# Turning the modulation rows of a two-block transformer kernel to columns once per eight steps

## The chip, the cores and the metric

The kernel runs on one core of one Trainium2 chip. The metric is the device time of one execution in microseconds (us); three executions were timed. Five engines work side by side: TensorE (PE, with its weight loads shown apart as PEld), VectorE (DVE), ScalarE (ACT), GpSimd (POOL) and SyncE (SP), which issues all the DMAs that matter here.

## What is computed

Block 1 has two layers over two streams, x (256 tokens) and ctx (256 tokens), each token 1024 wide. Each layer first makes six vectors of 1024 numbers from a conditioning vector; they scale, shift and gate the layer's two halves. There is one such set for each stream:

```
mx = jnp.split((silu_c @ w_mod[l] + b_mod[l])[:, None, :], N_MOD, axis=-1)
mc = jnp.split(silu_cc @ w_mod[l] + b_mod[l], N_MOD, axis=-1)
zx = modulate(rms_norm(x, norm1_g[l]), mx[0], mx[1]) @ w_in[l]
zc = modulate(rms_norm(ctx, norm1_g[l]), mc[0], mc[1]) @ w_in[l]
...
x = x + mx[2] * mixer_rest(fx, gx, attn_x, l)
hx = modulate(rms_norm(x, norm2_g[l]), mx[3], mx[4])
x = x + mx[5] * channel_mlp(hx, l)
```

`w_mod[l]` is 1024 x 6144, so per layer this product reads 25 MB of weights for only two rows of results (c and c_ctx). Between these lines stand an attention over eight heads, a Fourier mix, a convolution and an MLP. Block 2 (three mixers, a cross attention and an FFN) follows; it has no modulation.

## The kernel before

**Activations** lie with features on the 128 partitions and tokens along the free dimension. A large product goes block by block: 128 output features by 512 tokens, over eight k-tiles of 128, each in three passes (`wh`, `wh`, `wl`), because the weights and the activations are split into two parts each. ACT makes the high part of a weight block (`wh<-raw`), DVE the low part (`wl<-raw,wh`). Weight chunks of 512 KB land in four slots named `raw`, which the modulation weights share.

**Modulation** (`modulation`) is a generator of 24 steps per layer. A step is 128 features of two of the six vectors (256 columns in all), and eight steps make a pair of vectors, numbered r = 0, 1, 2. Here the weights are the moving operand: for each k-tile, a stationary `cs[:, k, :]` of 32 columns (columns 0 and 1 hold silu(c) and silu(c_ctx), the rest are zero) multiplies 256 columns of `raw`. The k-tiles go to four column groups of the array, so the partial sums of c and c_ctx lie on rows 32g and 32g + 1 of the accumulator `md`, half of a PSUM bank; the two halves alternate from step to step. A step's work is 8 matmuls of the program (16 in the trace, since fp32 goes in two passes), named `md<-raw,cs`. Then comes its **end**: ACT copies the half to `mrow` (`mrow<-md`), PE multiplies `mrow` as the stationary operand by the selector `sel`, which sums the four partial sums and turns rows to columns (`md<-cst_a,mrow`, 2 matmuls of the program, 4 in the trace), and DVE adds the bias (`mod<-md,vec`). The end writes into the half of `md` that it came from, and the step after next reuses that half. An end is written out after the next step's products.

**Order.** Ten steps are placed by hand around layer 0's first norm. From then on `weave` picks, by a model of when each engine is free, the next piece of several generators: keys and values, queries, attention, Fourier, convolution, input projection and, last, the filler, which is the modulation (in layer 1 alternating with the memory's keys and values for block 2). The traced program then goes through a list scheduler, which moves instructions again. `need_mod` forces the steps that are left before a vector is used: `need_mod(l, 2)` ahead of the output projection, and `need_mod(1, 0)` ahead of the last quarter of layer 0's MLP.

All engine instructions are recorded by one helper, so the profile gives every one of them line L238, and groups are told apart by tile names.

Of the kernel before, what the change touches and what calls it, by code (L numbers as in the profile page):

```python
# [11 lines left out]
F32 = mybir.dt.float32  # L12
# [15 lines left out]
# ------------------------------------------------------------------ layouts  # L28


def pack_w(w, kt, mc):
    """[kt*128, M] -> [M/mc, 128, mc/128 * kt * 128]: chunks that load contiguously, output block by block."""
    m = w.shape[1]
    return np.ascontiguousarray(
        w.reshape(kt, P, m // mc, mc // P, P).transpose(2, 1, 3, 0, 4).reshape(m // mc, P, kt * mc)
    )


def cols(v):
    """A vector of n*128 -> [128, n]."""  # L40
    return v.reshape(-1, P).T


def feat(a):
    """[T, D] -> [128, D/128, T]."""
    return a.T.reshape(-1, P, a.shape[0]).transpose(1, 0, 2)


def constants():
# [3 lines left out]
    sel = np.zeros((P, 2))  # L53
    for i in range(2):
        sel[i::32, i] = 1.0
# [88 lines left out]
INS = "ckv kr g0 a0 cq0 cq1 g1 a1 zf0 zf1".split()  # order of the blocks of w_in  # L144


def layout(i):
    """All device arrays, laid out; and where each small vector lies."""
# [72 lines left out]
# ------------------------------------------------------------------ program  # L221


TICK = 10.24 / 3  # of the PE's activity monitor, in us


class Engine:
    """An engine whose instructions the model of the core notes as they are issued."""
# [13 lines left out]
class Pool:  # L242
    """A tile pool whose slots' reuse the model notes."""
# [19 lines left out]
class Core:  # L263
    """The core, with a model of when each engine gets to what has been issued, in us.

    It serves only to choose the order in which work that does not depend on each other is traced."""
# [3 lines left out]
    TAIL = {"pe": 0.19, "dve": 0.16, "act": 0.18, "pool": 0.2, "dma": 2.0}  # until others see an end  # L270

    def __init__(self, nc):
# [3 lines left out]
        self.columns = {}  # tick of the PE's activity monitor -> columns counted  # L276
        self.used = {}    # tile -> end of its last use
        self.seen = {}    # tile -> accesses: box, end, engine, whether written
        self.last = 0.0   # the latest end since it was set to 0
        self.gaps = {k: [] for k in self.clock}  # when an engine waits, which later work may use  # L280
# [5 lines left out]
    def box(ap):  # L286
        """The first and last partition and element that an access touches."""
# [4 lines left out]
    def product(self, start, name, n, rows, cols, f32):  # L292
        """How long a product takes: the PE runs at half its rate after a tick with too few columns."""
# [28 lines left out]
    def after(self, ap):  # L322
        """When what has been issued so far has written ap."""
# [7 lines left out]
    def cooling(self):  # L331
        """Whether the PE has too few columns in this tick so far to run at its full rate in the next."""
# [3 lines left out]
    def place(self, key, ready, held):  # L336
        """When an instruction starts that could at ready: in the first gap that holds it, or behind the last."""
# [47 lines left out]
class Chain:  # L385
    """Work that is traced in steps: a generator that stops before products that wait for other engines.

    It yields the tiles that the next product waits for, nothing if that is all of the step, or a chain that has to
    end first. A chain that is mostly the DVE's (dve) goes on when the DVE has nothing else."""
# [6 lines left out]
class Squares:  # L396
    """Sums of squares over the features of tiles that come one by one: all but the last are added up on the way."""
# [18 lines left out]
    def sums(self, ones="ones"):  # L416
        """-> PSUM, the sums on each partition."""
# [7 lines left out]
class Early:  # L425
    """A norm's input before the norm, x times the scale of its features: both parts, tile by tile.

    The first products of a norm's output go on these; their sums take the norm's factor of each token (r) at the
    end, and with it the product of the shift."""
# [16 lines left out]
    def width(self, n):  # L446
        """How many columns its products of n tokens have: one stream's take the shifts along."""
        return n if self.shift is None or self.n > T else n + 2

    def shifts(self, blocks, pss):  # L450
        """The products of the shift with blocks of weights."""
# [33 lines left out]
class Prog:  # L485
# [28 lines left out]
    def later(self, tile, after):  # L514
        """Have the load of a tile wait for after: what is needed first goes first."""
# [23 lines left out]
    def banks(self, name, **bufs):  # L539
        """PSUM's banks, by use."""  # L540
# [5 lines left out]
    def temps(self, name, nhl, ntmp, nt):  # L546
        """Slots for plain activations ([128, nt]) and for activations' parts."""
# [10 lines left out]
    # ---- weights: load, split into the part that one pass carries and the rest  # L558
    @contextmanager
    def weights(self, name, nraw, wraw, nw=3, side="left"):  # L560
        """Slots for weights as loaded and for their parts."""
# [4 lines left out]
    def norms(self, name, n, side="left"):  # L566
        """Slots for norms of n tokens."""
# [14 lines left out]
    def wsplit(self, src, kt, f, wide=P, own=None):  # L582
        """-> (k, j) -> the two parts of the 128 x wide block of k-tile k and output block j."""
# [31 lines left out]
    def mm3(self, out, lh, ll, rh, rl, start, stop, **kw):  # L615
        """One K-tile of an fp32 product: three passes over exact parts."""
# [5 lines left out]
    def jobs(self, w, kt, mc, rhs, n, evac, chunks=None, m0=0, lead=0, kg=1, own=None, early=None, more=0, lead2=0,  # L622
             tag="mm"):
        """out^T[m] = sum_k W[k, m]^T act^T[k]; rhs: k -> (hi, lo). The first chunks (lead) go through k together,
        those of an Early and more of them on its tiles, and then lead2 ones.
# [1753 lines left out]
```

## Time and profile before

| | us |
|---|---|
| median of three executions (1748.15 to 1751.82) | 1751.02 |
| span of the profiled execution, first to last instruction | 1750.8 |
| PE busy in that span | 1667.3 |
| DVE busy | 1158.8 |
| ACT busy | 853.1 |
| mean granted TensorE clock, share of full speed | 0.962 |

The profiled execution has its span alone; no separate time for it is on record, and its span lies within the three times. It divides into stages: the start with the first norm (0 to 78 us), layer 0's projection and attention (78 to 252), its output projection and MLP (252 to 654), layer 1's projection and attention (654 to 820), the memory, output projection and MLP of layer 1 (820 to 1070), the mixers of block 2 (1070 to 1400), and the rest. Stage borders are rounded.

### The profile page before, as it was taken

How to read it: one execution, taken by the hardware profiler on the slowest of the kernel's cores; microseconds unless marked ns; L12 is line 12 of the kernel's file. 1: busy time of each engine (PE TensorE's matmuls, PEld its weight loads, DVE VectorE, ACT ScalarE, POOL GpSimd, SP SyncE). 2: the span in 40 equal slices, each digit the busy share in tenths (PEclk: the TensorE clock that was granted, in tenths of full speed). 3: DMA queues.
4: the chain of work that ended last, by engine and by line, in shares of the span. 5: the costliest groups of instructions: out<-in, count | busy, mean ns of one | idle time of the engine just before them, and what ended most of it. 6: DMA issues, size and time to landing. Idle time of an engine off the chain costs nothing.

```text
span 1750.8 us, 29987 instructions
## 1 busy us (share of the span) xinstructions
PE 1667.3 (95%) x12072; PEld 1429.8 (82%) x12072; DVE 1158.8 (66%) x2155; ACT 853.1 (49%) x1485; POOL 81.1 (5%) x74
## 2 busy tenths in 40 slices
PE   5899999999999998999999998899999999999997
PEld 3666668788888886767999997797888899999997
DVE  4686547743444366884679667787853868788864
ACT  4426764441323245466564446542334746666643
POOL 0000001000000011000100001011000001010000
PEclk8989999999999998989999998999988999999999
DMA  8743562233333335752756564332211475345553
GB/s 276 236 150 126 180 205 85 85 97 96 96 97 96 115 98 168 238 168 70 223 150 185 184 187 149 106 105 66 67 61 49 137 250 192 112 154 192 167 164 105
DMA packets 69403, 248.94 MB, mean 142 GB/s; under 512 B 7696, under 2 KB 13072, under 8 KB 65424
## 3 DMA queue, kind: packets, MB, share of 16 engines
q1 hardware_dynamic: 69264, 247.03, 44.2%
q8 instruction: 95, 1.56, 0.4%
q14 instruction: 44, 0.36, 0.1%
HBM read 242.80 MB, written 4.19 MB: 141 GB/s over the span
## 4 chain that ended last, share of the span: by engine, by line
PE 83%; DVE 8%; DMA 4%; ACT 4%; issue 1%; POOL 0%; SPq 0%; DVEq 0%; ACTq 0%
PE mm L238 63%; PE ax L238 11%; PE md L238 3%; PE sc L238 3%; PE fx L238 3%; DVE wl L238 2%; DMA raw<-w_in 1%; ACT wh L238 1%; DMA raw<-w_mod 1%; DVE tmp L238 1%; DVE y L238 1%; ACT L238 1%; DVE hl L238 1%; DMA x<-xc 0%; DVE x L238 0%
## 5 line engine op out<-in xcount | busy, mean ns | idle before, releaser
L238 PE MATMUL mm<-hl,wh 128*128 128x256 f32 (+2 forms) x3856 | 867.5, 320 | 15.0 <-DVE rw_in L238 7.6
L238 PEld LDWEIGHTS mm<-hl,wh 128*128 128x128 f32 x3856 | 645.5, 194 | 76.1 <-issue 8.7
L238 ACT CAST wh<-raw 128x1024 fp32r<-128x1024 f32 (+1 forms) x353 | 360.8, 1024 | 558.1 <-PE mm L238 434.3
L238 PE MATMUL mm<-hl,wl 128*128 128x256 f32 (+1 forms) x1928 | 613.4, 319 | 3.9 <-DVE wl L238 3.8
L238 DVE TENSOR_TENSOR wl<-raw,wh 128x1024 fp32r<-128x1024 f32 (+1 forms) x353 | 422.3, 1198 | 223.9 <-ACT wh L238 221.8
L238 PEld LDWEIGHTS mm<-hl,wl 128*128 128x128 f32 x1928 | 372.8, 193 | 30.4 <-DVE wl L238 6.8
L238 PE MATMUL mm<-y,wh 128*128 128x256 f32 x928 | 176.5, 290 | 7.1 <-DVE early L238 2.6
L238 PEld LDWEIGHTS mm<-y,wh 128*128 128x128 f32 x928 | 147.7, 194 | 10.3 <-DVE early L238 3.0
L238 PE MATMUL mm<-y,wl 128*128 128x256 f32 x464 | 133.1, 287 | 0.0
L238 DVE SCALAR_TENSOR_TENSOR x<-mm,mod,x 128x256 f32<-128x256 f32 x120 | 54.3, 480 | 117.9 <-PE mm L238 117.8
L238 POOL TENSOR_TENSOR sq<-sq,sq 128x256 f32<-128x256 f32 (+1 forms) x48 | 59.9, 1249 | 899.7 <-ACT sq L238 899.4
L238 PEld LDWEIGHTS mm<-y,wl 128*128 128x128 f32 x464 | 89.7, 193 | 0.6 <-issue 0.5
L238 PE MATMUL md<-raw,cs 128*32 128x256 f32 x768 | 62.6, 424 | 20.0 <-DMA raw<-w_mod 11.4
L238 PE MATMUL mm<-hid,wh 128*128 128x512 f32 x256 | 80.7, 397 | 0.0
L238 DVE SCALAR_TENSOR_TENSOR acc<-u,vec,acc 128x512 f32<-128x512 f32 (+1 forms) x120 | 73.2, 614 | 2.2
L238 ACT ACT_TABLE_LOAD x49 | 62.9, 1283 | 4.7 <-DMA vec<-vec 3.6
L238 PEld LDWEIGHTS md<-raw,cs 128*32 128x32 f32 x768 | 20.4, 115 | 48.6 <-issue 11.4
L238 PEld LDWEIGHTS mm<-hid,wh 128*128 128x128 f32 x256 | 48.2, 188 | 11.7
L238 PE MATMUL mm<-hid,wl 128*128 128x512 f32 x128 | 50.7, 396 | 0.0
L238 DVE TENSOR_REDUCE mx<-sc 128x1 f32<-128x512 f32 (+1 forms) x56 | 32.1, 574 | 24.5 <-PE sc L238 24.1
L238 PE MATMUL sc<-k,hl 96*128 96x512 f32 (+1 forms) x144 | 46.0, 420 | 1.4 <-ACT prob L238 1.4
L238 ACT CAST hl<-tmp 128x256 fp32r<-128x256 f32 (+1 forms) x62 | 28.7, 470 | 28.0 <-DVE tmp L238 27.8
(377 smaller groups left out, 2089.6 us busy)
## 6 DMA issues: line engine op xcount, KB each, us to landing
raw<-w_mlp SPq DMA_DIRECT2D x128, 512.0 KB, 3.6
raw<-w_mod SPq DMA_DIRECT2D x96, 512.0 KB, 4.7
raw<-w_up SPq DMA_DIRECT2D x22, 1024.0 KB, 4.9
raw<-w_gate SPq DMA_DIRECT2D x24, 512.0 KB, 3.6
raw<-w_down SPq DMA_DIRECT2D x16, 704.0 KB, 4.1
raw<-w_in SPq DMA_DIRECT2D x20, 512.0 KB, 4.7
raw<-w_o SPq DMA_DIRECT2D x16, 512.0 KB, 4.0
raw<-w_rw SPq DMA_DIRECT2D x14, 512.0 KB, 3.6
```

The source lines that it names most:

```text
L238: return f(out, *args, **kw)
```

## The change

Groups of eight steps share one half of `md`. Step q of a group uses a stationary operand shifted by 2q columns: `cs` is now 46 columns wide with the two live columns at 14 and 15, and the slice `14 - 2q : 46 - 2q` puts c and c_ctx on rows 2q and 2q + 1 of each 32-row group, zeros elsewhere. All eight steps accumulate in the same half (`start` only in the first, `stop` only in the last), and one end turns 16 rows to columns with a 16-column `sel`. Only layer 0's r = 0, which is needed first, keeps one end per step.

```
-    sel = np.zeros((P, 2))
-    for i in range(2):
+    sel = np.zeros((P, 16))
+    for i in range(16):
...
-        def end(at, row, ps):
+        def end(f0, m, r, row, ps):
             for h in range(2):
-                nc.tensor.matmul(ps[:, 2 * h:2 * h + 2], row[:, h * P:h * P + P], self.c("sel"), start=True, stop=True)
-            r, f = at // KD, at % KD
-            nc.vector.tensor_add(mv[:, r, :, f, :], ps[:, 0:4].rearrange("p (h i) -> p h i", i=2),
-                                 bm[:, r, :, f].unsqueeze(2).to_broadcast([P, 2, 2]))
+                nc.tensor.matmul(ps[:, 32 * h:32 * h + 2 * m], row[:, h * P:h * P + P], self.c("sel")[:, :2 * m], start=True,
+                                 stop=True)
+            nc.vector.tensor_add(mv[:, r, :, f0:f0 + m, :],
+                                 ps[:, 0:64].rearrange("p (h f i) -> p h f i", h=2, i=2)[:, :, :m, :],
+                                 bm[:, r, :, f0:f0 + m].unsqueeze(3).to_broadcast([P, 2, m, 2]))
...
-        for at in range(24):
-            ps = ps2[:, at % 2, :]
+        groups = [(at, 1) for at in range(KD)] if l == 0 else [(0, KD)]
+        groups += [(KD, KD), (2 * KD, KD)]
+        for gi, (at0, m) in enumerate(groups):
+            ps = ps2[:, gi % 2, :]
+            for at in range(at0, at0 + m):
...
-                nc.tensor.matmul(ps[32 * g:32 * g + 32, :], self.cs[:, k, :], raw[k // 4][:, k % 4 * T:k % 4 * T + T],
-                                 start=k < 4, stop=k >= 4, tile_position=(0, 32 * g))
-            row = self.c1.tile([P, T], F32, tag="mrow", bufs=2, name=self.nm("mrow"))
-            nc.scalar.copy(row, ps)
+                    nc.tensor.matmul(ps[32 * g:32 * g + 32, :], self.cs[:, k, 14 - 2 * q:46 - 2 * q],
+                                     raw[k // 4][:, k % 4 * T:k % 4 * T + T], start=q == 0 and k < 4,
+                                     stop=q == m - 1 and k >= 4, tile_position=(0, 32 * g))
+                if q == m - 1:
+                    row = self.c1.tile([P, T], F32, tag="mrow", bufs=2, name=self.nm("mrow"))
+                    nc.scalar.copy(row, ps)
...
-            self.cs = self.c1.tile([P, KD, 32], F32, name="cs")
+            self.cs = self.c1.tile([P, KD, 46], F32, name="cs")
             nc.vector.memset(self.cs, 0.0)
-            nc.scalar.activation(self.cs[:, :, 0:2], cc, AF.Silu)
+            nc.scalar.activation(self.cs[:, :, 14:16], cc, AF.Silu)
```

Since `weave` goes by its model, fewer ends also change what it picks. Three places matter below.

The first place is SP's queue in layer 0's input projection: the loads of the projection's weights (`w_in`), of the query weights (`w_uq`) and of the modulation weights (`w_mod`), in the order in which SP issues them. Before:

```order
L238 DMA raw_721<-w_in 128x1024
L238 DMA raw_759<-w_mod 128x1024
L238 DMA raw_771<-w_mod 128x1024
L238 DMA raw_776<-w_mod 128x1024
L238 DMA raw_788<-w_mod 128x1024
L238 DMA raw_793<-w_mod 128x1024
L238 DMA raw_805<-w_mod 128x1024
L238 DMA raw_836<-w_in 128x1024
L238 DMA raw_872<-w_in 128x1024
L238 DMA raw_891<-w_mod 128x1024
```

And with the change:

```order
L238 DMA raw_698<-w_in 128x1024
L238 DMA raw_736<-w_mod 128x1024
L238 DMA raw_746<-w_mod 128x1024
L238 DMA raw_762<-w_in 128x1024
L238 DMA raw_804<-w_in 128x1024
L238 DMA raw_878<-w_uq 128x1024
L238 DMA raw_922<-w_mod 128x1024
```

Ahead of the projection's last two weight chunks stand two modulation loads now, where there were six.

The second place is PE in the second half of layer 0's attention (`sc` are scores, `ax<-cst_a,prob` transposes of probabilities, `mm<-pt,v` the values, `mm<-hl,wh` the queries of the next heads). Before, steps and ends of the modulation stand among them:

```order
L238 MATMUL md<-cst_a,mrow_1893 128x2 x2
L238 MATMUL ax_1851<-cst_a,prob_1773 128x128 x4
L238 MATMUL mm_1792<-pt_1790,v_596 64x128
L238 MATMUL md<-raw_1929,cs 32x256 x4
L238 MATMUL md<-raw_1972,cs 32x256
L238 MATMUL sc_1864<-k_959,hl_1541 128x256 x3
L238 MATMUL md<-raw_1972,cs 32x256 x3
L238 MATMUL ax_1870<-cst_a,prob_1801 128x128 x2
L238 MATMUL mm_1822<-hl_751,wh_1525 128x512 x2
```

With the change, the same part for the second-last pair of heads:

```order
L238 MATMUL sc_1739<-k_872,hl_1419 128x256 x3
L238 MATMUL ax_1745<-cst_a,prob_1661 128x128 x4
L238 MATMUL mm_1680<-pt_1678,v_564 64x128
L238 MATMUL sc_1775<-k_870,hl_1404 128x256 x3
L238 MATMUL ax_1781<-cst_a,prob_1695 128x128 x2
L238 MATMUL mm_1716<-hl_728,wh_1388 128x512 x2
```

No modulation stands there any more: in the changed program the attention's first two pairs of heads hold all of the stage's remaining steps, and its last two pairs hold none. The steps that are left (three in sum) move to the end of the MLP and to layer 1.

The third place is PE in layer 0's MLP, at the start of its last quarter (`mm<-hl,wh` is the down projection), where before no modulation stands at all. With the change:

```order
L238 MATMUL md<-raw_4523,cs 32x256 x4
L238 MATMUL mm_4554<-hl_4003,wh_4544 128x512 x2
L238 MATMUL mm_4554<-hl_4003,wl_4545 128x512
...
L238 MATMUL mm_4554<-hl_4256,wh_4544 128x512
L238 MATMUL md<-cst_a,mrow_4533 128x16 x2
L238 MATMUL mm_4554<-hl_4256,wh_4544 128x512
```

The half step that completes layer 1's first group stands there, and one block of products later the group's end, which `need_mod(1, 0)` asks for.

## Rows read from the trace of the kernel before

**Rows 1.** The page's first part: busy time, share of span, instructions.

```profile
PE 1667.3 (95%) x12072; PEld 1429.8 (82%) x12072; DVE 1158.8 (66%) x2155; ACT 853.1 (49%) x1485; POOL 81.1 (5%) x74
```

**Rows 2.** Windows by stage: us, busy by engine, clock, DMA share, GB/s.

```profile
core 0: us, PE busy (x) PEld busy (x) DVE busy (x) ACT busy (x) POOL busy (x), PEclk, DMA share, GB/s
78.00:252.00 174.00, 168.31 (x1121) 116.67 (x1121) 115.68 (x229) 97.73 (x210) 0.00 (x0) 0.95 0.49 161
325.00:654.00 329.00, 328.69 (x1437) 269.89 (x1437) 153.67 (x201) 107.33 (x144) 9.09 (x8) 1.00 0.33 101
654.00:820.00 166.00, 151.27 (x1065) 116.75 (x1064) 119.24 (x259) 97.36 (x190) 6.08 (x6) 0.91 0.49 161
1070.00:1400.00 330.00, 314.08 (x3095) 267.56 (x3096) 241.52 (x503) 152.44 (x245) 18.32 (x16) 0.92 0.30 91
```

**Rows 3.** Tile md: engine, operation, count, ns min/median/max, first and last start.

```profile
L238 PE MATMUL md<-raw,cs x768: 376/379/637, 8.3 to 780.8; 128*32 128x256 f32 x192
L238 PEld LDWEIGHTS md<-cst_a,mrow x192: 186/192/338, 21.8 to 788.2; 128*128 128x128 f32 x192
L238 PE MATMUL md<-cst_a,mrow x192: 165/251/374, 21.8 to 788.2; 128*128 128x2 f32 x192
L238 ACT COPY mrow<-md x48: 348/372/387, 10.7 to 781.3; 128x256 f32<-128x256 f32 x48
```

**Rows 4.** The same windows, instructions of tile mrow alone.

```profile
78.00:252.00 174.00, 12.15 (x88) 13.43 (x88) 8.09 (x22) 0.95 0.49 161
654.00:820.00 166.00, 8.71 (x60) 8.83 (x60) 5.21 (x14) 0.91 0.49 161
```

**Rows 5.** PE's timeline around one end: start us, us, instruction, count.

```profile
99.31 0.62 PE L238 MATMUL mm<-hl,wh 128*128 128x512 f32 x2
99.77 0.39 PE L238 MATMUL mm<-hl,wl 128*128 128x512 f32 x1
99.99 0.50 PE L238 MATMUL md<-cst_a,mrow 128*128 128x2 f32 x4
100.35 0.71 PE L238 MATMUL mm<-hl,wh 128*128 128x512 f32 x2
100.90 0.39 PE L238 MATMUL mm<-hl,wl 128*128 128x512 f32 x1
```

**Rows 6.** PE's timeline, 106 to 114 us; idle time before in brackets.

```profile
106.18 0.61 PE L238 MATMUL md<-cst_a,mrow 128*128 128x2 f32 x4 [0.49 <-ACT mrow L238]
108.80 1.94 PE L238 MATMUL md<-raw,cs 128*32 128x256 f32 x16 [2.02 <-DVE mod L238]
111.91 1.22 PE L238 MATMUL mm<-hl,wh 128*128 128x512 f32 x2 [1.18 <-ACT wh L238]
112.93 0.84 PE L238 MATMUL md<-cst_a,mrow 128*128 128x2 f32 x4
113.64 0.77 PE L238 MATMUL mm<-hl,wl 128*128 128x512 f32 x1
```

**Rows 7.** SP's timeline, 71 to 110 us: DMA issues, with the queue's waits.

```profile
71.38 2.86 SPq L238 DMA_DIRECT2D raw<-w_in  x2
74.34 31.30 SPq L238 DMA_DIRECT2D raw<-w_mod  x6
105.75 4.52 SPq L238 DMA_DIRECT2D raw<-w_in  x2
```

**Rows 8.** Windows, columns as above: two slow stretches, one pair of heads.

```profile
112.00:118.00 6.00, 6.00 (x16) 4.90 (x17) 6.00 (x9) 1.17 (x2) 0.00 (x0) 0.50 0.74 249
179.00:187.00 8.00, 7.13 (x30) 5.14 (x34) 4.31 (x10) 6.06 (x12) 0.00 (x0) 0.57 0.35 137
202.80:226.75 23.95, 23.95 (x210) 16.23 (x208) 11.95 (x31) 16.34 (x42) 0.00 (x0) 1.00 0.67 219
```

**Rows 9.** That pair of heads, instructions of tile md alone (no POOL column).

```profile
202.80:226.75 23.95, 7.98 (x96) 4.45 (x96) 0.65 (x4) 1.84 (x5) 1.00 0.67 219
```

**Rows 10.** PE's timeline: a wait in layer 0's attention, one in layer 1.

```profile
179.87 1.65 PE L238 MATMUL sc<-k,hl 96*128 96x512 f32 x3 [1.43 <-ACT prob L238]
...
685.46 1.08 PE L238 MATMUL md<-raw,cs 128*32 128x256 f32 x8 [2.82 <-DVE mod L238]
```

More of the change, by code (lines that the diff above doesn't have):

```diff
@@ L747, in half @@
             return self.raw(self.a[f"w_mod{l}"][at, :, i * 1024:i * 1024 + 1024], 1024)
-        for at in range(24):
-            self.mark(f"mod{l}")
-            raw = [raw or half(at, 0), half(at, 1)]
-            ps = ps2[:, at % 2, :]
-            for k in range(KD):
-                g = k % 4
-                nc.tensor.matmul(ps[32 * g:32 * g + 32, :], self.cs[:, k, :], raw[k // 4][:, k % 4 * T:k % 4 * T + T],
-                                 start=k < 4, stop=k >= 4, tile_position=(0, 32 * g))
-            row = self.c1.tile([P, T], F32, tag="mrow", bufs=2, name=self.nm("mrow"))
-            nc.scalar.copy(row, ps)
-            raw = half(at + 1, 0) if at < 23 else None
-            if last is not None:
-                end(*last)
-            last = at, row, ps
-            if at % KD == KD - 1:
-                yield [row]
-                self.mark(f"mod{l}")
-                end(*last)
-                last = None
-                self.mod_done[l] = at // KD + 1
-            yield [raw] if raw is not None else []
+        groups = [(at, 1) for at in range(KD)] if l == 0 else [(0, KD)]
@@ new lines, in modulation @@
+        groups += [(KD, KD), (2 * KD, KD)]
+        for gi, (at0, m) in enumerate(groups):
+            ps = ps2[:, gi % 2, :]
+            for at in range(at0, at0 + m):
+                self.mark(f"mod{l}")
+                raw = [raw or half(at, 0), half(at, 1)]
+                q = at - at0
+                for k in range(KD):
+                    g = k % 4
+                    nc.tensor.matmul(ps[32 * g:32 * g + 32, :], self.cs[:, k, 14 - 2 * q:46 - 2 * q],
[4 more added lines that the diff above has]
+                    nc.scalar.copy(row, ps)
+                raw = half(at + 1, 0) if at < 23 else None
+                if last is not None:
+                    end(*last)
+                    last = None
+                if q == m - 1:
+                    last = at0 % KD, m, at // KD, row, ps
+                if at % KD == KD - 1:
+                    yield [row]
+                    self.mark(f"mod{l}")
+                    end(*last)
+                    last = None
+                    self.mod_done[l] = at // KD + 1
+                yield [raw] if raw is not None else []
```

## The prediction

> **What bounds the kernel now.** The page's first part comes first: PE is busy for 1667.3 of 1750.8 us, no other engine above 66% [rows 1]. So PE is where time can be won, but a busy PE counts overlapping instructions, and a share over the whole span hides stages. The windows by stage come next [rows 2]: the MLP of layer 0 keeps PE busy for 328.69 of 329 us at full clock, so any PE instruction put there costs its full spacing. The two stages that hold the modulation are less dense: layer 0's projection and attention leave PE idle for 174 - 168.31 = 5.7 us, layer 1's for 166 - 151.27 = 14.7 us, with granted clocks of 0.95 and 0.91. What I read from these: in layer 0 PE's own work sets the time, with a few stalls; in layer 1 weight landings and DVE have a larger share. The third view is tile md by itself, for what a step and an end cost, and the fourth PE's timeline around single ends.
>
> **What is removed.** Each of the 48 steps has an end of four traced matmuls (192 in all), one ACT copy and one DVE add [rows 3]. Layer 0's first eight steps keep their ends; the other 40 get five. So 40 - 5 = 35 ends go. By place: 22 ends (88 / 4) stood in layer 0's stage and 15 (60 / 4) in layer 1's [rows 4], the other 11 before 78 us.
>
> The cost of one end on a dense PE is read from start to start, not from busy time [rows 5]. A product that follows the `wl` pass would start 0.22 us after it (0.39 long, but pipelined: the end itself starts 99.99 - 99.77 after). The end then holds the array until 100.35, so 0.36 us. The pair behind it takes 100.90 - 100.35 = 0.55 to its successor where the pair ahead took 99.77 - 99.31 = 0.46, so 0.09 more: 0.45 us per end. Lower bound: 0.36. Upper bound: at half clock an end takes 113.64 - 112.93 = 0.71 [rows 6]. I take 0.45, since the stages run at 0.91 to 0.95 of full clock. 35 x 0.45 = 15.8 us (bounds 12.6 and 24.9). The ACT copies (35 x 0.372 = 13.0 us) [rows 3] and the DVE adds lie beside PE; neither engine bounds a stage, so they count for nothing by themselves.
>
> The Trainium skill, Perfetto Trace Analysis, section Identifying the Most-Contended Engine, says that matmul busy time misjudges TensorE and that the busy time of LDWEIGHTS is the better measure. By the rule an end would be worth its four weight loads, 4 x 0.192 = 0.77 us, and the removed ends 26.9 us instead of 15.8, an estimate by that page. The spacing in [rows 5] shows less than that, so these loads run partly under the products ahead of them; the sum goes by the spacing.
>
> **What is added.** The five new ends have 16 moving columns, not 2. A traced fp32 matmul takes 0.251 us with 2 columns and 0.379 with 256 [rows 3], so 14 columns more are 0.128 x 14 / 254 = 7 ns, and for 20 matmuls 0.14 us at most. I take nothing. The stationary slices keep 32 columns, so the 768 matmuls of the steps cost what they did. The 14 further columns of `sel` and of `cs` per k-tile lie in the first 8 us, ahead of the first step at 8.3 us [rows 3]; without that cover the 112 columns more to clear cost less than a 256-column copy, 0.37 us [rows 3].
>
> **What is moved.** First, SP's queue: of the last projection weights, two chunks were issued behind six modulation loads, which took the queue from 74.34 to 105.75 us, because each waits for one of four slots [rows 7]. The late chunks then made PE wait 1.18 us for `wh`. Just ahead PE waited 0.49 for the row copy and 2.02 for the bias add of an end, together 3.7 us [rows 6], and then the clock stood at 0.50 for 6.00 us, at a cost of 3.0 us [rows 8]. With the change, steps of one group neither copy nor wait for a half to come free, so the two end waits have no cause, and only two modulation loads stand ahead of the chunks. Bounds: 0 (PE reaches the same landing sooner and waits there) and 6.7. I take the two end waits, 2.5, and half of the other 4.2, so 4.6. In layer 1, PE waited 2.82 us for the bias add once [rows 10], but DVE was held there behind weight parts whose load had just landed; a landing is not moved by this change, so I take 0, with 2.8 as the upper bound.
>
> Second, fillers: a bare pair of heads, read from the pair at 202.80, has 23.95 us of dense PE with five steps and four ends in it (96 matmuls) that keep PE busy for 7.98 [rows 8, 9], so 16.0 us of PE for the pair itself. ACT has 16.34 - 1.84 = 14.5 for it, DVE 11.95 - 0.65 = 11.3. PE stays the longest, so the bare pairs are shorter, but little slack covers the chain from scores through maximum, exponential and normalisation to the transposes. The trace has one stretch where that chain came late: a wait of 1.43 us [rows 10], then a granted clock of 0.57 over 8.00 us [rows 8]. That cost 1.43 + 8.00 x 0.43 = 4.9 us. Bounds for the two bare pairs: 0, and both at half clock throughout, 2 x 16.0 = 32.0 more. I take one such event, 4.9, the nearest row.
>
> Third, three steps go to the end of the MLP and to layer 1. Their products cost PE the same there, and their six loads fall on stages with a DMA share of 0.33 and 0.49 [rows 2]. In the MLP, ACT's copy stands behind one weight cast, and the end stands one block of products behind the step (8 k-tiles at 99.99 - 99.31 = 0.68 us for three passes [rows 5], 5.4 us), so PE should not wait; were that cover gone, at least a copy's length, 0.37 us. What would be late next is the first scaled tile of layer 1, which needs the end's result.
>
> Fourth, the model that orders block 2's mixers starts from another state, so equal work stands there in another order. The idle time of that stage is 330 - 314.08 = 15.9 us [rows 2]; a quarter of it either way, 4 us, is my bound, and I take 0.
>
> **Sum.** -15.8 - 4.6 + 4.9 = -15.5 us, from 1750.8 to 1735.3. The span is 0.2 us under the median of the timed runs, so in their terms 1735.5.
>
> **Rivals.** An effect of 0.2% (3.5 us) is about what a measurement of this kernel tells from none.
> - *The weight loads count in full.* In attention an end often stands between instructions shorter than a 512-column product, with less to hide its loads under; each then costs 4 x 0.192 = 0.77. The spacing of 0.36 plus 0.09 in [rows 5], beside 512-column products, speaks against it elsewhere. Time: 35 x 0.77 = 26.9, and -26.9 - 4.6 + 4.9 = -26.6, so 1724.4. It is the case of the rule that the Trainium skill states in Perfetto Trace Analysis.
> - *The ends were filler.* `weave` put them where PE would have waited anyway: in attention for ACT, in layer 1 for landings. Then only ends outside such gaps pay. For it: the 14.7 us idle in layer 1. Against it: PE busy in all of 23.95 us of the pair [rows 8]. If 25 of 35 were free and the stall at 106 us came back, 10 x 0.45 = 4.5 and the time is about 1746.5.
> - *The bare attention loses the clock*, which ends slower. Without steps between them, the last two pairs wait for ACT again and again; after a 1.43 us wait the clock fell in the trace, to 0.57 over the stretch. Each pair held at half clock costs 16.0 us. Two of them: -15.8 - 4.6 + 32.0 = +11.6, so 1762.6. It decides from 20.4 / 16.0 = 1.3 pairs on. Against it: PE's 16.0 exceeds ACT's 14.5, so ACT can keep up on average. The Trainium skill, TensorE: Matmul & The Clock Gate, section HAM oscillation, states that idle gaps between bursts make TensorE's clock fall back, again and again; the trace agrees in the stretch of 0.57.
>
> **How the numbers follow.** Likeliest, the sum: 0.57, own range 1729 to 1743. Weight loads in full: 0.12. Ends were filler: 0.22; its time lies at the border of the measurable, so a little over half of it still counts as faster. Bare attention slower: 0.09. Faster by over 0.2% (under 1747.5): 0.56 + 0.12 + 0.12 = 0.80. Within 0.2%: 0.11. Slower: 0.09. The range takes in the weight-load case and the filler case up to its border, and leaves out the slow one: 1724 to 1751.
>
> **What the profile after would show.** Ends: 52 traced `md<-cst_a,mrow` matmuls (13 ends), 13 copies. The stage from 78 us on some 15 us shorter, and its steps' waits for `mrow` and `mod` gone; the last two projection chunks issued well before 100 us. Bare pairs of 16 to 20 us, with waits for `prob` or `pt`. The MLP lengthened by about 1 us, with no PE wait at its new end. Block 2 within 4 us of before. What would make me wrong: long waits for ACT or a clock near 0.5 in the last two pairs; new waits for landings in layer 1, where loads stand in another order; or a shorter layer 0 whose gain layer 1 gives back.

## The result, and the profile after

The changed kernel takes 1774.74 us (median of 4 runs, 1769.26 to 1785.72), the kernel before 1749.78 in the same comparison: a ratio of 1.015, 95% interval 1.0111 to 1.0189. It is 25 us slower where I forecast 15 faster. The profiled execution spans 1772.9 us, 22.1 more than before.

PE's line in the page's first part has 140 instructions fewer than in [rows 1], and 6.2 us less busy time:

```profile
PE 1661.1 (94%) x11932; PEld 1413.0 (80%) x11932; DVE 1153.2 (65%) x2120; ACT 845.5 (48%) x1452; POOL 78.3 (4%) x74
```

The work is what the diff says. In the view of tile md (columns as in [rows 3]) there are 52 traced products of ends instead of 192, 13 copies instead of 48, and the steps' products cost what they did. The last line is from the same view's list of what ended the idle time ahead of these instructions: weight landings, 39 times for 38.2 us in all, where before it was 8 times for 16.1 us.

```profile
L238 PE MATMUL md<-raw,cs x768: 379/379/637, 7.9 to 789.4; 128*32 128x256 f32 x192
L238 PE MATMUL md<-cst_a,mrow x52: 165/251/353, 21.7 to 794.1; 128*128 128x2 f32 x32, 128*128 128x16 f32 x20
L238 ACT COPY mrow<-md x13: 347/373/394, 10.3 to 793.3; 128x256 f32<-128x256 f32 x13
...
  DMA raw<-w_mod: 38.2, 39
```

The windows of [rows 2] again, at the same times, after the change:

```profile
78.00:252.00 174.00, 162.25 (x1005) 105.49 (x1004) 115.06 (x210) 93.67 (x192) 0.00 (x0) 0.97 0.43 147
325.00:654.00 329.00, 329.00 (x1465) 268.86 (x1463) 152.56 (x203) 106.97 (x145) 9.12 (x8) 1.00 0.33 102
654.00:820.00 166.00, 139.93 (x992) 103.02 (x990) 111.68 (x235) 86.11 (x166) 4.40 (x6) 0.92 0.52 175
1070.00:1400.00 330.00, 309.24 (x3019) 262.24 (x3017) 229.51 (x473) 144.01 (x234) 23.16 (x21) 0.90 0.27 85
```

PE is idle for 11.8 us of the first window (5.7 before), 26.1 of the third (14.7) and 20.8 of the last (15.9). So there is less work, and more waiting than work was saved.

Where the time went is read from two landmarks of the chain of work that ended last (start us, us, instruction, count): the dense products that open layer 0's MLP, and the output projection of layer 1. In the kernel before:

```profile
325.55 329.17 PE mm L238 x1438
...
850.05 23.04 PE mm L238 x192
```

In the changed kernel, with the pieces between them that are waits for modulation weights in layer 1 (five; before, the chain has one such piece, of 5.93 us):

```profile
321.87 285.28 PE mm L238 x1246
...
714.92 4.56 DMA raw<-w_mod
...
723.32 5.45 DMA raw<-w_mod
...
734.62 3.80 DMA raw<-w_mod
...
765.60 6.75 DMA raw<-w_mod
...
779.24 5.15 DMA raw<-w_mod
...
866.51 23.04 PE mm L238 x192
```

Up to the MLP 3.7 us are won (325.55 to 321.87). From there to layer 1's output projection 20.1 are lost (850.05 - 325.55 = 524.50 before, 866.51 - 321.87 = 544.64 after), and 5.6 behind it (900.75 to 906.39, to the end of the span). The sum is 22.0.

PE's waits from 654 to 840 us, the largest first (total us, times, longest). The wait for `hl` is that of layer 1's first key-value product, and e1 below, which is faster than before, has it too (5.0 us); what sets the changed kernel apart is the waits for `w_mod` and for `acc`, the convolution's sums:

```profile
PE md L238 <- DMA raw<-w_mod: 9.3, 9, 3.2
PE mm L238 <- ACT hl L238: 7.8, 1, 7.8
PE ax L238 <- DVE acc L238: 6.0, 1, 6.0
PE ax L238 <- ACT acc L238: 3.2, 1, 3.2
```

PE's timeline shows where the last two stand: at the end of layer 1's attention, behind its last products with the values.

```profile
821.55 1.22 PE L238 MATMUL ax<-acc,cst_a 128*128 128x256 f32 x2 [6.00 <-DVE acc L238]
823.74 1.22 PE L238 MATMUL ax<-sq,cst_a 128*128 128x256 f32 x2 [0.96 <-ACT sq L238]
...
833.12 2.08 PE L238 MATMUL ax<-acc,w_pw 128*128 128x256 f32 x4 [3.21 <-ACT acc L238]
```

In block 2 one wait is new, for a masked product of the RWKV mixer that stands behind the S5 scan on DVE:

```profile
1266.16 1.97 PE L238 MATMUL ax<-rw_m,rw_in 64*64 64x64 f32 x32 [7.65 <-DVE rw_m L238]
```

### The profile page after: what moved, and what is told of

It is laid out like the page before. It is cut to its first block, busy times and chain, and to the rows that moved or that the text cites. A ratio compares the mean times of both kernels' runs of the same rounds, so it can differ in the third digit from the quotient of the medians.

```text
span 1772.9 us, 29588 instructions
## 1 busy us (share of the span) xinstructions
PE 1661.1 (94%) x11932; PEld 1413.0 (80%) x11932; DVE 1153.2 (65%) x2120; ACT 845.5 (48%) x1452; POOL 78.3 (4%) x74
## 4 chain that ended last, share of the span: by engine, by line
PE 81%; DVE 8%; DMA 5%; ACT 4%; issue 2%; SPq 0%; POOL 0%; ACTq 0%; DVEq 0%
PE mm L238 62%; PE ax L238 11%; DMA raw<-w_mod 3%; PE md L238 3%; PE sc L238 2%; PE fx L238 2%; DVE wl L238 2%; DVE tmp L238 1%; ACT wh L238 1%; DMA raw<-w_in 1%; DVE y L238 1%; DVE hl L238 1%; ACT L238 1%; DVE s_z L238 0%; ACT prob L238 0%
## 5 line engine op out<-in xcount | busy, mean ns | idle before, releaser
L238 PE MATMUL md<-raw,cs 128*32 128x256 f32 x768 | 66.7, 411 | 24.2 <-DMA raw<-w_mod 14.0
L238 PEld LDWEIGHTS mm<-hid,wh 128*128 128x128 f32 x256 | 48.1, 188 | 11.7
L238 ACT COPY rw_in<-ax 128x64 f32<-128x64 f32 (+2 forms) x34 | 12.7, 415 | 63.0 <-PE ax L238 61.8
```

Of the source, the lines that this page charges most:

```text
L238: return f(out, *args, **kw)
```

## The experiments

Theory A: the removed ends are worth what I said, and the loss comes from the order. `weave` keeps a model of the core and picks the next chain by it; with no ends to charge for, the model's clock runs otherwise and all later choices change. Theory B: the summing of eight steps in one half costs time itself. Theory C: the ends were worth nothing.

**Replaying the order (e1 to e5).** The sequence of chains that `weave` picked in either kernel was written into a table, by weave (0 and 1 are the layers, 2 and 3 block 2), and replayed:

```diff
         live = list(chains)
+        plan, at = PLAN.get(self.woven, ""), 0
+        self.woven += 1
...
+            if at < len(plan):
+                c = chains[int(plan[at])]
+                at += 1
             self.mark(c.phase)
```

e1_old_order, the changed kernel with all four sequences of before. 

> The change's arithmetic, with `weave` replaying, choice by choice, the sequence of chains that it took in the kernel before (in both layers and in both weaves of block 2). Nothing else differs from the changed kernel. Theory A (the order is what costs): the removed ends are worth the 35 x 0.45 = 15.8 us of the prediction, and all of the loss comes from where `weave` puts work when its model no longer charges for ends; then about 1735 us, 1728 to 1742. Rival B (the summing itself costs: eight steps wait on one PSUM half, or read a strided stationary more slowly): the order changes nothing, 1770 to 1780. Rival C (ends were worth nothing, and the order costs what was lost): 1747 to 1753.

e2_old_order_layer0, only weave 0 of before. 

> The changed kernel, with the choices of the kernel before replayed in layer 0 alone; layer 1 and block 2 replay the changed kernel's own choices. The output projection of layer 0 begins 3.5 us earlier in the changed kernel than before, where the ends that were removed up to there (about 33) should give 33 x 0.45 = 14.9. Theory A: those 11 us come back, and the time is 1774.7 - 11 = 1764, 1758 to 1768. Rival B: 1770 to 1780.

e3_old_order_layer1, only weave 1 of before. 

> The changed kernel, with the choices of the kernel before replayed in layer 1 alone; layer 0 and block 2 replay the changed kernel's own choices. From the start of layer 1's scores to the drained rest of the memory's values the changed kernel takes 15.6 us more. Theory A: these come back, and some 5 us of removed ends with them: 1774.7 - 18 = 1757, 1752 to 1762. Rival B: 1770 to 1780.

e4_before_new_order, the kernel before with the four sequences of the changed one. 

> The kernel before, arithmetic and all its 48 ends untouched, with the sequence of choices that `weave` takes in the changed kernel. Theory A: the order alone costs the whole loss and the ends on top of it, 1774.7 + 15.8 = 1790, 1780 to 1800. Rival B: the order costs nothing, 1747 to 1755. Rival C: 1770 to 1778.

e5_old_order_block2, only weaves 2 and 3 of before. 

> The changed kernel, with the choices of the kernel before replayed in the two weaves of block 2 alone; layers 0 and 1 replay the changed kernel's own choices. From the first DVE work of block 2's mixers to the dense stretch at the end, the changed kernel takes 7.1 us more than the kernel before (510.97 against 503.88). Order theory: these come back, 1774.7 - 7 = 1768, 1763 to 1772. Rival (the loss there is carried over from layer 1, by loads that start late): 1772 to 1778.

All kernels of this study, in us. The stages are read from the two landmarks above in each one's chain; ratios are to runs of before on the same chip.

| kernel | median | ratio, 95% interval | to the MLP | MLP to layer 1's output projection | from there to the end |
|---|---|---|---|---|---|
| before | 1749.78 | | 325.55 | 524.50 | 900.75 |
| changed | 1774.74 | 1.015 [1.0111, 1.0189] | 321.87 | 544.64 | 906.39 |
| e1_old_order | 1743.61 | 0.9968 [0.9938, 0.9998] | 324.81 | 519.36 | 897.43 |
| e2_old_order_layer0 | 1762.04 | 1.0076 [1.0051, 1.0102] | 322.26 | 531.98 | 901.36 |
| e3_old_order_layer1 | 1763.06 | 1.0062 [1.0034, 1.009] | 324.54 | 526.99 | 910.57 |
| e4_before_new_order | 1769.87 | 1.0109 [1.0081, 1.0137] | 316.20 | 548.04 | 905.96 |
| e5_old_order_block2 | 1767.24 | 1.0092 [1.0059, 1.0125] | 327.39 | 545.22 | 896.19 |
| e6_paced_old_order | 1738.41 | 0.9931 [0.9901, 0.9961] | 322.55 | 519.65 | 897.20 |
| e7_paced | 1771.97 | 1.0105 [1.0055, 1.0155] | 315.06 | 546.56 | 899.98 |
| e8_before_double_ends | 1770.74 | 1.0103 [1.0049, 1.0157] | 341.35 | 526.00 | 900.45 |
| e9_conv_early | 1763.05 | 1.0087 [1.0055, 1.0119] | 324.01 | 529.20 | 899.29 |
| e10_half_loads | 1766.66 | 1.0105 [1.0071, 1.0138] | 323.73 | 536.53 | 900.04 |
| e11_half_steps | 1741.67 | 0.9952 [0.9924, 0.998] | 323.85 | 520.66 | 888.89 |
| e12_deeper | 1734.5 | 0.9924 [0.9898, 0.995] | 326.31 | 517.34 | 900.15 |
| e13_before_deeper | 1755.34 | 1.0035 [1.0006, 1.0064] | 332.89 | 521.28 | 905.03 |
| e14_three_back | 1767.78 | 1.0107 [1.0072, 1.0143] | 327.51 | 535.92 | 904.37 |

The first stage differs by up to 5.5 us between kernels with the same order in it (changed, e3, e5, e9, e10: 321.87 to 327.39), the second by 0.6 (changed and e5) and 1.0 (e6 and e11, which differ in layer 0 alone), the last by up to 16 (with the old order in block 2: 888.89 in e11, 905.03 in e13). So medians and the second stage carry the argument; a difference of 3 us in the first, or of 6 in the last, shows nothing.

The stages come from one profiled execution of each kernel, and some of these lie off the median: e7 8.6 us below it, e9 8.8, e11 6.5, e2 4.7, e10 4.6; e13 5.7 above it, e12 11.1. The medians are those of 4 to 10 executions. The intervals of e1, e2, e3, e6, e11 and e12 lie apart from the changed kernel's; those of e4, e5, e7, e9, e10 and e14 overlap with it. The slowest execution of e9 (1765.70) is still faster than the fastest of the changed kernel (1769.26); those of e5 (1756.73 to 1776.06) don't part from it.

The order costs 31 us (changed against e1), and the same order costs the kernel before 20 (e4). B falls: with the old order the changed kernel is the faster one. A is right about the cause and too high about the gain: 1743.6 lies just above its range, between it and C's. In e4 A's gain is missing altogether: 1769.87 lies at the border of C's range, 10 us below A's, and in the new order the kernel without ends is the slower one by 4.9 us (the intervals overlap). Replayed one at a time, layer 0, layer 1 and block 2 give back 12.7, 11.7 and 7.5 us; e2 and e5 came out within their ranges, e3 1.1 us above its own. That the three add up to 31.9, the whole loss, rests on block 2's 7.5, which isn't clear of noise.

But layer 0's share isn't won in layer 0. e2 reaches the MLP no earlier than the changed kernel (322.26 and 321.87); its gain is in the next stage, 544.64 to 531.98, with layer 1's own choices unchanged. That led to e14.

**What an end costs (e8).** Each end of the kernel before issues its products twice:

```diff
-                nc.tensor.matmul(ps[:, 2 * h:2 * h + 2], row[:, h * P:h * P + P], self.c("sel"), start=True, stop=True)
+                for _ in range(2):
+                    nc.tensor.matmul(ps[:, 2 * h:2 * h + 2], row[:, h * P:h * P + P], self.c("sel"), start=True, stop=True)
```

> The kernel before with its own choices replayed, and every one of its 48 ends issues its two products twice into the same columns: 192 traced matmuls more on PE, no copy, no add and no wait more. If an end costs the 0.45 us of the prediction: 1749.5 + 48 x 0.45 = 1771, 1766 to 1776. If its weight loads count in full (0.77): 1786. If ends mostly fill what PE would wait for anyway: 1750 to 1758.

20.2 us for 48 ends, 0.42 each: the forecast's 0.45. The chain says where: the MLP begins at 341.35, 15.8 later than before, and the second stage is longer by 1.5 only. The Trainium skill, Perfetto Trace Analysis, section Identifying the Most-Contended Engine, gives MFU (the share of the peak arithmetic rate) and the busy share of LDWEIGHTS as the measures of how near TensorE is to its limit. The forecast's rival read that as a price, 0.77 us an end; this run shows about half of that.

**Spacing (e6, e7).** In e4 the ends still stand between the steps, in the changed kernel they don't, and the scheduler that orders each engine's queue pulls the steps ahead. The row of the steps' products, from 60 to 254 us (last start behind "to"), in e4:

```profile
L238 PE MATMUL md<-raw,cs x336: 378/380/637, 64.0 to 229.7; 128*32 128x256 f32 x168
```

and in the changed kernel:

```profile
L238 PE MATMUL md<-raw,cs x336: 379/379/405, 63.7 to 191.4; 128*32 128x256 f32 x168
```

The same choices, and layer 0's last step runs 38 us earlier, with half of attention left bare; the MLP begins at 316.20 in e4 and at 321.87 to 327.39 without ends. e6 and e7 spread the steps again by their loads, e6 with the old order, e7 without a table:

```diff
+        if after is not None:
+            self.later(w, after)
...
-            return self.raw(self.a[f"w_mod{l}"][at, :, i * 1024:i * 1024 + 1024], 1024)
+            return self.raw(self.a[f"w_mod{l}"][at, :, i * 1024:i * 1024 + 1024], 1024, self.pace)
...
+            self.pace = st[max(t - 4, 0)].get("p")
```

e6_paced_old_order. 

> As e1_old_order, and each load of modulation weights traced during attention first waits for the probabilities of four units of attention earlier (one DVE copy of a column per load). In e1 the choices are those of the kernel before, but without ends a step waits for nothing but its load, and the scheduler that orders each engine's queue lets the last step of layer 0 run beside the 48th of the 96 score products, where before it ran beside the 96th; behind it PE was idle for 3.2 of 20 and 4.0 of 25 us (200 to 245 us). Paced, the last step stands beside the 96th again. Pacing theory (the ends also spread the steps, and the bare half of attention is what is left of the loss): those 7 us come back, about 1737, 1731 to 1741. Rival (ends were mostly filler, and the gain of e1 is all there is): 1741 to 1748.

e7_paced. 

> The changed kernel with its own choices, and the loads of modulation weights paced as in e6_paced_old_order. Pacing theory: layer 0 gets back what replaying the old choices there gave or more (12.7 us), while layer 1's convolution and block 2 stay as the changed kernel has them or move with the model's clock: 1755 to 1766. Rival (which choices `weave` makes is all that matters, pacing is nothing): 1770 to 1778.

e6 came to 1738.4, within the expected range, but its trace doesn't bear out the reason: the first stage is 2.3 us shorter than in e1, inside the spread, and the intervals of e1 and e6 overlap. e7 missed its range and fell into the rival's. Its MLP begins at 315.06, some 7 to 12 earlier than in the changed kernel's order and about where e4 has it, which speaks for the spacing in the first stage; but the second stage is as long as in the changed kernel (546.56). It isn't the same layer 1: without a table `weave` chose anew, and e7's waits from 654 to 840 us have none for `acc` and 6.1 us for landings. Why it lost as much, I did not settle.

**Layer 0: work or chain (e11 to e13).** PE's window from 130 to 250 us, layer 0's attention (columns as in [rows 2]), before the change:

```profile
130.00:250.00 120.00, 117.99 (x865) 79.97 (x864) 68.71 (x159) 82.25 (x187) 0.00 (x0) 0.97 0.52 171
```

in e1:

```profile
130.00:250.00 120.00, 110.40 (x757) 67.65 (x754) 66.86 (x138) 74.66 (x163) 0.00 (x0) 0.97 0.51 171
```

and in e6:

```profile
130.00:250.00 120.00, 110.09 (x779) 65.57 (x777) 68.05 (x173) 76.08 (x167) 0.00 (x0) 0.99 0.52 176
```

PE's busy time fell by 7.6 and 7.9 us (16 of 18 ends, and about 1.7 and 1 of 18 steps, are gone from the window) and its idle time rose by as much, from 2.0 to 9.6 and 9.9, at a clock no lower, whether the steps stood early or were spread. So something else holds the stage. The score products of the whole attention, before and in the changed kernel (first and last start around "to"), say the same: it began 10.7 us earlier and ended where it did.

```profile
L238 PE MATMUL sc<-k,hl x96: 274/391/804, 140.8 to 245.2; 96*128 96x512 f32 x48, 96*128 96x256 f32 x48
L238 PE MATMUL sc<-k,hl x96: 274/389/796, 130.1 to 245.4; 96*128 96x512 f32 x48, 96*128 96x256 f32 x48
```

e11 takes out more work:

```diff
-                for k in range(KD):
+                nk = 4 if self.attending else KD
+                for k in range(nk):
```

> As e6_paced_old_order, but the 18 modulation steps traced during layer 0's attention issue only four of their eight products: half of each sum is left out, so the output is not the reference's; loads, copies and ends stay. By the pair of before (7.98 us of PE for five steps and four ends, 0.45 an end) a step is 1.24 us of PE, so 18 half steps are 11.2 us less work there. PE theory (attention is bound by PE's work): 1738.4 - 11 = 1727, 1723 to 1732. Latency theory (PE's work ends just at what the chain from scores to maximum, exponential, transposes and values allows, so that work taken out turns into waits for ACT): layer 0 gains under 4 us, 1734 to 1742.

e12 and e13 give the chain of a unit one step more, in e6 and in the kernel before:

```diff
-            yield from self.pipeline(len(units), ((1, probs), (0, scores), (2, turn), (3, values)),
+            yield from self.pipeline(len(units), ((1, probs), (0, scores), (3, turn), (4, values)),
```

e12_deeper. 

> As e6_paced_old_order, and in the pipeline over the units of attention the transposes and the products with the values come one step later, so that maximum, exponential and normalisation of a unit have two steps of other units' work above them and not one. Latency theory: most of PE's 10 us of waits in layer 0's attention (130 to 250 us) and some of layer 1's go, 1738.4 - 8 = 1730, 1725 to 1734. PE theory, or waits that have another cause (landings): 1736 to 1742.

e13_before_deeper. 

> The kernel before with its own choices replayed, and the deeper pipeline of e12_deeper in both layers. PE is idle for 2.0 us of layer 0's attention (130 to 250 us) there, so by the latency theory there is little to win: 1746 to 1751. If the deeper pipeline gains as much here as in e12, the waits that it removes have nothing to do with the removed ends: 1740 to 1744.

The window in e11:

```profile
130.00:250.00 120.00, 104.11 (x619) 64.94 (x617) 66.20 (x170) 74.26 (x163) 0.00 (x0) 0.89 0.51 171
```

Another 6.0 us of busy time gone, 6.0 more idle, the granted clock down from 0.99 to 0.89, and the MLP begins at 323.85, no earlier than in e6. The modulation's own products take 12.8 us less in the window (25.54 to 12.76), so by these figures about half of what was taken out went into other work at the lower clock and half into idle time. The PE theory falls: the median, 1741.67, lies in the latency theory's range, and work taken out of this stage buys nothing. The Trainium skill, TensorE: Matmul & The Clock Gate, section HAM oscillation, says that idle gaps between bursts let the clock fall back; e11 agrees, while in e1 and e6 some 10 us of idle time left it at 0.97 and 0.99.

Which chain holds the stage stays open. e12 won 3.9 us against e6 with overlapping intervals, and its trace, of an execution 11.1 us above the median, can't say where; e13 missed both of its ranges, slower than before by 7.35 (1755.34 against 1747.99). Waits for modulation weights, which the kernel before doesn't have in this window, are the largest group of PE's waits there in e6 and in e11 (total us, times, longest):

```profile
PE md L238 <- DMA raw<-w_mod: 3.0, 3, 1.7
PE md L238 <- DMA raw<-w_mod: 4.8, 5, 1.5
```

Whether these landings hold the stage, no run tests: e10 below halves the loads of layer 1 alone.

**Layer 1: convolution, landings, moved steps (e9, e10, e14).** Three single edits of the changed kernel, whose own choices are otherwise replayed. e9 moves the convolution's steps (4) among those of layer 1 (2 is attention, 6 the filler):

```diff
-    1: "012345600555555555666600000255455454514516255555446656645233344663226263233444462266622662622666224444444444446224444624462442262466664644",
+    1: "012356005555555556666000002555555151644425555566566544444444444233366322626344442336226662266262266644444444444422644442262624226266666444",
```

> The changed kernel with its own choices replayed everywhere, and in layer 1 only the steps of the convolution moved, to where the kernel before has them, counted in steps of attention (its second half at 15 of 27 steps and not at 17 to 21). In the changed kernel the last DVE tap of layer 1's convolution starts at 821.0 us, before at 788.3, and at the end of attention PE waits 6.0 + 1.0 + 3.2 us for the convolution's sums, squares and output. Convolution theory: that is the larger part of layer 1's loss of 11.7 us, and these 10 us go: 1774.7 - 10 = 1765, 1761 to 1769. Landing theory (PE's nine waits for modulation weights, 9.3 us, are the loss; what is won at the end is waited for elsewhere): 1771 to 1777.

e10 halves the modulation loads of layer 1:

```diff
-                raw = [raw or half(at, 0), half(at, 1)]
+                raw = [raw or half(at, 0)]
+                raw.append(raw[0] if l and at >= KD else half(at, 1))
```

> The changed kernel with its own choices replayed everywhere; in layer 1 each of the remaining modulation steps loads only the first half of its weights and takes it for both halves, so that half of these transfers and of their slots is gone and the output is not the reference's; PE has as many products as before. Landing theory: most of PE's 9.3 us of waits for modulation weights in layer 1 go, 1774.7 - 8 = 1767, 1763 to 1770. Convolution theory: DVE's taps end as late as they did, so PE waits for them longer at the end of attention and little is won, 1771 to 1776.

e14 puts four filler calls back into layer 0's sequence:

```diff
-    0: "60123450605560000025545544545144516255444544545454452633622333244444444623222662232622323444444462264442262426664224266246226226262262262222",
+    0: "601234506055600000255455445451445162554445445454544526336223332444444446232226622326223234444444622644422624266642242662462626226626226622626222",
```

> The changed kernel with its own choices replayed everywhere, and four calls of the filler more in layer 0's attention (behind its steps 28, 31, 34 and 37), so that the three and a half modulation steps that the change had moved to the end of the MLP and to layer 1 stand in layer 0 again; pacing, convolution and block 2 stay as in the changed kernel. Moved-steps theory (layer 0's attention is bound by its chain and has room, layer 1 has not, so the three steps cost there far more than their 1.24 us of PE; with the old choices in layer 0 alone layer 1 took 10 us less): layer 0 not longer by more than 2, layer 1 about 10 shorter, 1774.7 - 10 = 1765, 1760 to 1769. Rival (a step costs PE its 1.24 us wherever it stands): 1771 to 1777.

Of e9, the row of the convolution's taps, whose last starts at 793.6 now and not at 821.0,

```profile
L238 DVE SCALAR_TENSOR_TENSOR acc<-u,vec,acc x60: 459/476/486, 716.6 to 793.6; 128x256 f32<-128x256 f32 x60
```

and the first of PE's waits from 654 to 840 us:

```profile
PE md L238 <- DMA raw<-w_mod: 10.9, 10, 2.3
```

The waits for `acc` are gone from the list, those for landings stay, and the second stage is 15.4 us shorter (529.20), 2.2 from that of e3, which replays layer 1's whole old order. Part of the 15.4 is the clock: from 640 to 845 us it is 0.96 in this execution, the fastest of its four, and 0.90 in the changed kernel's. By the medians e9 and e3 win the same, 11.7 us. So the convolution's place is nearly all that layer 1's own order costs.

In e10 the waits for `w_mod` are gone from the head of the list, and those for the convolution stay:

```profile
PE ax L238 <- DVE acc L238: 5.0, 1, 5.0
...
PE ax L238 <- ACT acc L238: 3.2, 1, 3.2
```

The second stage is 8.1 us shorter, so the landings cost as well; that what is won is waited for at the end was wrong. In e14 it is 8.7 shorter, for 2.5 steps less in it (216 traced products from 640 to 845 us against 256), and the waits for landings are 3.7 instead of 9.3:

```profile
PE md L238 <- DMA raw<-w_mod: 3.7, 3, 2.4
```

By the stage that is 3.5 us a step where it costs PE 1.24. The first stage, with the steps back in it, takes 327.51, the upper end of its spread, and the median falls by 7.0. Both medians, of e10 and of e14, lie within the ranges of the landing and the moved-steps theory, but their intervals overlap with the changed kernel's.

**Block 2.** The wait of 7.7 us for `rw_m` (7.7 to 7.8) is in the traces of the changed kernel, e3, e4 and e14, whose last stage takes 904.4 to 910.6 us. It isn't in those of e2, e9 and e10 (899.3 to 901.4), which replay the same choices, so the scheduler behind `weave` decides it as well; nor in e5, whose median is 7.5 us lower. But e13, with the old order and 1.7 us of this wait, takes 905.03, and the intervals of e5 and the changed kernel overlap. What block 2's order costs is not shown.

## Why the prediction was wrong

The sum had 15.5 us to win; the changed kernel lost 25. The step that failed is the move of work into layer 1, which the forecast took at next to nothing: three steps that "cost PE the same there", "a landing is not moved by this change, so I take 0", and no term for the order of the rest. The second stage, where this falls, takes 544.64 us instead of 519.36 with the old order, 25.3 more: the convolution late behind attention (11.7 by the median of e9), the moved steps and their landings (7.0 and 8.1 by those of e14 and e10); these overlap and don't add. Beside it, a term was mis-sized: the ends of layer 0.

- **What is removed:** the price of an added end was sized rightly, 0.42 us by doubling beside 0.45. The forecast needed what its removal gives. With the old order 13 ends of layer 1 are gone and the second stage gained 5.1 us (524.50 to 519.36; forecast 13 x 0.45 = 5.9). 22 are gone ahead of layer 0's MLP (33 of 48 stood there, 11 of 13 are left; e2's expectation counted all 33), and the first stage gained 0.7 to 3.3 (e1, e2 and e6; forecast 9.9), inside its spread, although the stall of the next item is gone there too. There the rival that the ends were filler was right, and the argument against it, a PE busy in all of the pair's 23.95 us [rows 8], was the error: a stage can have PE full and another chain just under it.
- **The stall at 106 us** went, and whole, where the forecast took 4.6 of 6.7 us. SP issued the two late projection chunks in a row that begins at 82.74 us, behind only two modulation loads (the queue of [rows 7] after the change), and PE, idle for 3.7 us from 78 to 130 us before, is busy throughout at full clock (second view, columns as in [rows 2]). Either half of the change does this: PE is busy for all of these 52 us in e4, with the new order and all its ends, and for 51.95 in e1, with the old order and without them. But most of what was won here did not reach the MLP: attention began earlier and ended no earlier.

```profile
73.59 2.25 SPq L238 DMA_DIRECT2D raw<-w_mod  x2
82.74 5.37 SPq L238 DMA_DIRECT2D raw<-w_in  x2
```

```profile
78.00:130.00 52.00, 52.00 (x256) 38.29 (x255) 42.05 (x61) 17.15 (x24) 0.00 (x0) 1.00 0.40 131
```

- **Fillers, second of the moves:** "PE stays the longest, so the bare pairs are shorter", with one event of 4.9 us, fell. Bare or not, layer 0's attention did not get shorter with PE's work: its score products stretch over 115.3 us, 104.4 before. The slower rival was not what happened either: the granted clock was 0.80 from 200 to 225 us and 1.00 from there to 250, not half:

```profile
200.00:225.00 25.00, 20.63 (x95) 13.23 (x94) 13.38 (x28) 18.62 (x35) 0.00 (x0) 0.80 0.00 1
225.00:250.00 25.00, 22.52 (x145) 14.88 (x140) 9.28 (x25) 17.53 (x47) 0.00 (x0) 1.00 0.06 22
```

- **Three steps moved:** "Their products cost PE the same there" is what failed most plainly: by e14 they cost 8.7 us in the second stage instead of 2.5 x 1.24 = 3.1, in large part waits for their own landings (9.3 against 3.7).
- **Layer 1's order** has no term in the sum. I priced the waits seen before and took 0; that the convolution would end 32.7 us later on DVE, behind attention, cost 11.7 by the medians of e9 and the changed kernel. The forecast asked what becomes of PE's waits and SP's loads, and not what DVE still owes PE when the stage ends.
- **Block 2:** the bound of 4 us had no ground but a quarter of the idle time. One wait of 7.7 came in, and from layer 1's output projection to the end the kernel took 5.6 us more, which lies inside that stage's spread; so the runs don't say whether the bound was broken.

What would make the forecast wrong named two of these: landings in layer 1, and a gain of layer 0 that layer 1 gives back. They had no price and no chance.

The change with the old order and paced loads, e6, beats both kernels (0.9931), and so does e12 (0.9924); the runs don't tell these two apart. e6 is 12.1 us faster than before, where the forecast had 15.5 for the change itself.

## What to carry to other kernels

Price removed work by removing it: take out as much or more in a trial, and see whether the stage gets shorter, before a cost read from spacing is multiplied by a count. Where a planner or scheduler sets the order, replay the old order with the new arithmetic; the two effects had opposite signs here, and the order's was the larger. Small dependent work between fillers also spaces them, so when it goes, ask what will hold them back, and read the ends of the chains on every engine in the new order, DVE's too.

## What was not expected of the hardware

Taking 18 half steps out of a stage with PE busy for 110 of 120 us lowered its clock from 0.99 to 0.89 and left its length as it was (e11 against e6, one trace each). An end of four products cost 0.48 us in layer 0 when doubled (15.8 / 33) and 0.1 in layer 1 (1.5 / 15), while taking ends out gave the reverse: 0.03 to 0.15 us each in layer 0 (0.7 to 3.3 for 22), 0.39 in layer 1 (5.1 / 13). The first stage's figures carry its spread of 5.5 us. Why layer 1 answers so, no run here shows.
